# The MLP of a hybrid encoder block: three of its four two-chunk products by seven block products, activations kept in DRAM

## The chip, the cores and the metric

One core of a Trainium2 chip runs the kernel. The metric is the device time of one execution in microseconds (us), lower is better. The kernel before takes 2594.95 us, the median of three runs (2592.05 to 2595.93).

## The reference, cut to what matters

One encoder layer on 2048 rows of width 1024, all in float32. The last line of the block, the MLP, is what changes:

```python
h = rmsnorm(x, norm_mix_g); proj = h @ w_in                  # 1024 -> 5 x 512: q, k, v, u, vg
a_out = stick_breaking_attention(q, k, v)                    # 8 heads of 64, strictly causal
b_out = spatial_gating(gelu(u), gelu(vg), ...)               # 128-row blocks
mix = concat(rmsnorm(a_out), rmsnorm(b_out))
x = x + mix @ w_out                                          # 1024 -> 1024
h = rmsnorm(x, norm_mlp_g)
act = square(relu(h @ w_up))                                 # 1024 -> 4096
x = x + act @ w_down                                         # 4096 -> 1024
return rmsnorm(x, norm_final_g)
```

## The kernel before

The 2048 rows go in four chunks of 512 (`TC`). Every product keeps float32 accuracy by splitting both operands into a high and a low part: `split` (lines 78 to 85) makes the high part on ACT (lines 81, 84) and the low part, the difference, on DVE (lines 82, 85), and `mm3` (lines 87 to 90) issues three matmuls per 128x128 by 128x512 block:

```python
def mm3(ps, lh, ll, rh, rl, first, last):
    nc.tensor.matmul(ps, lh, rh, start=first, stop=False)
    nc.tensor.matmul(ps, lh, rl, start=False, stop=False)
    nc.tensor.matmul(ps, ll, rh, start=False, stop=last)
```

The program has four kinds of work. `proj` (line 108) makes q, k, v and the gated rows of a chunk and writes q, k and v to DRAM. Its layer-norm part multiplies and adds on POOL (GpSimd, lines 225 and 226). `attention` (line 280) is a generator of 325 steps. Step i forms the scores of a block of 128 queries and 512 keys (PE, lines 309 and 310), two sigmoids (ACT, 315 and 317), a scan and a product (DVE, lines 320 and 321 on the diagonal, 323 and 324 off it), and for earlier blocks four transposes (PE, 334), a split of the transposed weights `aT` and two products with v (PE, 352 and 353). 128 of its 320 blocks are on the diagonal and shorter. The third kind is the class `Block` (line 398): `out_operands` and `out` (the output projection, rows of x added on DVE at line 478), `turn` (line 491: RMS norm, then transposes into `hT`), and the MLP by `up` (line 507) and `down` (line 543).

The MLP of a chunk goes by 16 groups of 256 hidden columns. `up` loads the weights of a group, splits them, multiplies them with `hT` (24 matmuls per 128 hidden columns), and leaves the split activations in SBUF; `down` multiplies them at once with `w_down` and adds the products to the rows `y` on DVE (line 557). Nothing of the MLP goes through DRAM. `middle` (line 588) chains them.

The order around the change is written out at the end of the function (lines 638 to 686) with `together(main, side, ratio)`: `side`, the attention, moves `ratio` steps for each step of `main`, a step being 12 matmuls of a product.

```python
together(proj([0, 1], [here, Rows(spx, ps_x, "x", 0)], sp, True))
...
together(proj([2], [here], sp, False), side, R_A)      # R_A = 0.65
together(proj([3], [here], sp, True), side, R_A)
...                                                    # out and turn of chunk 0 and 1: R_O = 0.8
last = together(blocks[0].middle(), side, R_B)         # R_B = 1.0
...
assert together(middle, side, R_B) is OPEN             # the attention ends inside chunk 1's MLP
...                                                    # chunks 2 and 3 then share one Block and its weights
```

So chunk 0 and a part of chunk 1 run their MLP beside the attention, and chunks 2 and 3 run theirs together afterwards. Loads and stores are issued on SP's queue (`nc.sync`). Each engine's instructions are put in order when the program is built; tiles of one name share a fixed number of buffers (`bufs`).

## Time and profile before

| | |
|---|---|
| median of three runs | 2594.95 us (2592.05 to 2595.93) |
| the profiled execution: first to last instruction (span) | 2591.2 us; the page gives no other time for it |
| instructions | 33154 |
| DMA | 299.99 MB, mean 116 GB/s |

A share in the page is busy time over the span, averaged over stages that differ. A matmul's listed time is its latency; matmuls overlap, so the distance between two starts is what one costs. Windows (stretches of the span) show for each engine the busy time and, in brackets, the number of instructions, then the granted TensorE clock as a share of full speed, the busy share of the DMA engines, and GB/s.

### The profile page before, as it was taken

What the parts mean: (1) busy time and instruction counts of PE and PEld (TensorE: products, weight loads), DVE (VectorE), ACT (ScalarE), POOL (GpSimd) and SP (SyncE); (2) the same over time, 40 slices, a digit from 0 to 9 for tenths busy, and PEclk for the clock granted to TensorE, in tenths of its full rate; (3) what the DMA queues carried; (4) which work ended last, traced back from release to release, by engine and by line L of the source; (5) the groups of instructions that cost most, each with busy time, mean ns of one, the idle gap of its engine ahead of it and who ended that gap; (6) DMA issues with size and microseconds to landing.
All of it is one profiled execution on the core that took longest, in us unless ns stands there. A gap on an engine that the chain in (4) does not pass through costs nothing.

```text
span 2591.2 us, 33154 instructions
## 1 busy us (share of the span) xinstructions
PE 2521.4 (97%) x11904; PEld 2047.3 (79%) x11904; DVE 1795.8 (69%) x2722; ACT 1223.2 (47%) x2306; POOL 164.4 (6%) x175
## 2 busy tenths in 40 slices
PE   7999998999999999999999999999999999999998
PEld 5788776777878888777788888877888888888886
DVE  6634688778888888899888888875833434344445
ACT  6314456455556555565655555663533232222222
POOL 3200022010000000011000000011100000000000
PEclk9999999999999999999999999999999999999999
DMA  6246756556443444346343334343311111111111
GB/s 211 97 127 207 217 158 193 155 175 192 130 123 118 122 123 122 122 123 196 98 121 116 117 117 122 108 145 98 131 54 47 46 49 49 49 49 45 45 45 66
DMA packets 160229, 299.99 MB, mean 116 GB/s; under 512 B 16576, under 2 KB 32960, under 8 KB 160064
## 3 DMA queue, kind: packets, MB, share of 16 engines
q1 hardware_dynamic: 155760, 295.77, 37.1%
q10 hardware_dynamic: 4304, 2.10, 0.3%
q8 instruction: 94, 1.54, 0.3%
q14 instruction: 71, 0.58, 0.1%
HBM read 255.86 MB, written 41.94 MB: 115 GB/s over the span
## 4 chain that ended last, share of the span: by engine, by line
PE 70%; DVE 20%; DMA 3%; issue 3%; ACT 3%; POOL 1%; SPq 0%; DVEq 0%; POOLq 0%; ACTq 0%
PE mm L89 20%; PE mm L90 20%; PE mm L88 20%; DVE pr L323 4%; DVE y L557 3%; PE tr L334 3%; DVE aT L82 2%; DVE b L324 2%; PE av L352 2%; PE av L353 2%; PE z L309 1%; PE z L310 1%; DVE pr L320 1%; DMA st<-in_w_in 1%; DVE w L82 1%
## 5 line engine op out<-in xcount | busy, mean ns | idle before, releaser
L81 ACT ACTIVATE w<-w_st 128x512 fp32r<-128x512 f32 x384 | 242.7, 634 | 457.1 <-PE mm L90 442.9
L82 DVE TENSOR_TENSOR w<-w_st,w 128x512 fp32r<-128x512 f32 x384 | 259.9, 685 | 163.8 <-ACT w L81 163.7
L90 PE MATMUL mm<-hT,w 128*128 128x512 f32 (+1 forms) x816 | 309.7, 379 | 0.0
L89 PE MATMUL mm<-hT,w 128*128 128x512 f32 (+1 forms) x816 | 308.7, 378 | 0.0
L88 PE MATMUL mm<-hT,w 128*128 128x512 f32 (+1 forms) x816 | 308.6, 378 | 0.1
L88 PE MATMUL mm<-w,act 128*128 128x512 f32 x768 | 300.8, 392 | 2.1 <-DVE y L557 1.4
L90 PE MATMUL mm<-w,act 128*128 128x512 f32 x768 | 301.6, 393 | 0.0
L89 PE MATMUL mm<-w,act 128*128 128x512 f32 x768 | 300.6, 391 | 0.0
L557 DVE TENSOR_TENSOR y<-mm,y 128x512 f32<-128x512 f32 x384 | 257.7, 684 | 49.9 <-PE mm L90 49.3
L323 DVE TENSOR_TENSOR_SCAN pr<-kk,pr,zeros 128x513 f32<-128x513 f32 x192 | 245.4, 1279 | 33.8 <-ACT kk L315 33.7
L315 ACT ACTIVATE kk<-z 128x512 f32<-128x512 f32 (+2 forms) x320 | 168.7, 527 | 176.4 <-PE z L310 122.3
L535 ACT ACTIVATE rl<-mm 128x512 f32<-128x512 f32 x128 | 76.5, 597 | 327.1 <-PE mm L90 326.9
L82 DVE TENSOR_TENSOR aT<-tr,aT 128x512 fp32r<-128x512 f32 (+1 forms) x320 | 190.7, 596 | 6.9 <-ACT aT L81 6.9
L334 PE MATMUL tr<-ident,b 128*128 128x128 f32 x1088 | 180.2, 275 | 6.1 <-DVE b L324 2.6
L81 ACT ACTIVATE aT<-tr 128x512 fp32r<-128x512 f32 (+1 forms) x320 | 172.7, 540 | 21.0 <-PE tr L334 20.4
L88 PEld LDWEIGHTS mm<-hT,w 128*128 128x128 f32 x816 | 154.0, 189 | 30.3 <-DVE y L557 0.5
L82 DVE TENSOR_TENSOR act<-rl,act 128x512 fp32r<-128x512 f32 x96 | 65.8, 686 | 161.0 <-ACT act L81 159.9
L90 PEld LDWEIGHTS mm<-hT,w 128*128 128x128 f32 x816 | 153.5, 188 | 29.4
L89 PEld LDWEIGHTS mm<-hT,w 128*128 128x128 f32 x816 | 153.5, 188 | 29.2
L88 PEld LDWEIGHTS mm<-w,act 128*128 128x128 f32 x768 | 144.6, 188 | 36.2 <-DVE y L557 3.7
L317 ACT ACTIVATE b<-z 128x512 f32<-128x512 f32 (+2 forms) x320 | 169.9, 531 | 0.0
L90 PEld LDWEIGHTS mm<-w,act 128*128 128x128 f32 x768 | 144.1, 188 | 31.3
(185 smaller groups left out, 5272.0 us busy)
## 6 DMA issues: line engine op xcount, KB each, us to landing
w_st<-in_w_up SPq DMA_DIRECT2D x192, 256.0 KB, 2.8
w_st<-in_w_down SPq DMA_DIRECT2D x192, 256.0 KB, 2.8
kt<-k_d SPq DMA_DIRECT2D x160, 256.0 KB, 4.7
st<-in_w_in SPq DMA_DIRECT2D x60, 512.0 KB, 5.2
vt<-v_d SPq DMA_DIRECT2D x80, 256.0 KB, 3.0
w_st<-in_w_out SPq DMA_DIRECT2D x64, 256.0 KB, 3.4
st<-in_x_t SPq DMA_DIRECT2D x16, 512.0 KB, 4.8
st<-in_x SPq DMA_DIRECT2D x16, 512.0 KB, 4.8
```

The costliest lines, as they stand in the source:

```text
L81: nc.scalar.activation(hi, src, AF.Copy)
L82: nc.vector.tensor_tensor(lo, src, hi.bitcast(F32), ALU.subtract)
L88: nc.tensor.matmul(ps, lh, rh, start=first, stop=False)
L89: nc.tensor.matmul(ps, lh, rl, start=False, stop=False)
L90: nc.tensor.matmul(ps, ll, rh, start=False, stop=last)
L315: nc.scalar.activation(kk[:, :L], z[:, :L], AF.Sigmoid, scale=-QK_SCALE)
L317: nc.scalar.activation(b[:, :L], z[:, :L], AF.Sigmoid, scale=QK_SCALE)
L323: nc.vector.tensor_tensor_scan(pr[:, ::-1], kk[:, ::-1], zeros, carry[tb], ALU.mult, ALU.add)
L324: nc.vector.tensor_tensor(b, b, pr[:, 1:TC + 1], ALU.mult)
L334: nc.tensor.transpose(tr[:, tb * P:(tb + 1) * P], bs[tb][:, j * P:(j + 1) * P], ident)
L535: nc.scalar.activation(rl, ps, AF.Relu)
L557: nc.vector.tensor_tensor(y[:, hs], ps, y[:, hs], ALU.add)
```

## The change

The MLP works on two chunks at once (0 and 1, then 2 and 3). Of its four products, the up product of chunks 0 and 1 stays as it was (`up_plain`, beside the attention); the down product of chunks 0 and 1 and both products of chunks 2 and 3 are made from seven block products on a 2x2 split of both operands, instead of eight, with sums of blocks formed before (`seven`, `seven_left`) and after (on PSUM results). The activations' seven block operands are written to DRAM (`s_d`) and read back for `down_seven`; so are the rows `y` (`y_d`), `hT` of chunks 2 and 3 (`h_d`) and its sums (`th_d`). The attention's rates change, and it now ends inside `up_plain`.

```diff
-    R_A, R_O, R_B = 0.65, 0.8, 1.0
+    R_A, R_O, R_U = 1.0, 1.0, 1.75
...
-    FG, RL_BUFS, ST_BUFS, W_BUFS = 2, 2, 4, 9
-    class Block:      # out_operands, out, turn, up, down, middle
...
+    NG = 4
+    ORDER = (0, 5, 6, 4, 1, 3, 2)
+    ORDER_D = (0, 5, 1, 6, 4, 3, 2)
+    class Out:        # operands, product, turn: as before, in fewer and larger pieces; y goes to y_d
...
+    def seven(rm, b11, b12, b21, b22, spare):
+        t1, t2, t4n = spare
+        nc.gpsimd.tensor_tensor(t1, b12, b11, ALU.subtract)
+        nc.gpsimd.tensor_tensor(t2, b22, t1, ALU.subtract)
+        nc.gpsimd.tensor_tensor(b12, b22, b12, ALU.subtract)
+        nc.gpsimd.tensor_tensor(t4n, b21, t2, ALU.subtract)
+        return [b11, b21, b22, t4n, t1, t2, b12]
+    def seven_left(engine, a11, a12, a21, a22, spare):
+        s1, s2, s4 = spare
+        engine.tensor_tensor(s1, a21, a22, ALU.add)
+        engine.tensor_tensor(s2, s1, a11, ALU.subtract)
+        engine.tensor_tensor(a21, a11, a21, ALU.subtract)
+        engine.tensor_tensor(s4, a12, s2, ALU.subtract)
+        return [a11, a12, s4, a22, s1, s2, a21]
+    def keep_acts(p, q, a11, a12, a21, a22, rm, engine):
+        ops = seven_left(engine, a11, a12, a21, a22, ...)
+        for i, op in enumerate(ops):
+            nc.sync.dma_start(s_d[p][q // 4][i][:, q % 4, :], op)
+    def up_plain(p, hTs, rm):
+        for q in range(16):
...                    # 2 x (load, split) of w_up, 4 x 24 matmuls, relu, square
+            keep_acts(p, q, ..., rm, nc.gpsimd)
+    def sums_of_h(rm):
+        for j in range(4):
+            st = rm.raw8([2, 2, TC])
+            nc.sync.dma_start(st, h_d[j])
+            ops = seven(rm, ...)
+            for i in range(4):
+                nc.sync.dma_start(th_d[i][:, j, :], ops[3 + i])
+    def up_seven(p, rm):
+        for i in ORDER:
+            st = rm.raw8([4, TC])          # from h_d or th_d, split into hc[i] = rm.big([2, 4, TC])
...
+        for q in range(16):
+            st = rm.raw8([2, 2, 512])
+            nc.sync.dma_start(st, w_up[2 * q:2 * q + 2]...)
+            ops = seven_left(nc.gpsimd, ...)
...                    # 7 forms: split of ops[i], 12 matmuls; 5 additions on DVE from PSUM; relu, square
+            keep_acts(p, q, c11, c21, c12, u3, rm, nc.vector)
+    def down_seven(p, rm):
...                    # y of both chunks (y_d) and an accumulator stay in rm.big
+        for g in range(NG):
+            for h in range(2):
+                st = rm.big([4, D])
+                nc.sync.dma_start(st, w_down[f0 * P:(f0 + 4) * P, :]...)
+                ops.append(seven(rm, ...))                # operands of 128x1024
+            for n, i in enumerate(ORDER_D):
+                st = rm.raw8([4, TC])
+                nc.sync.dma_start(st, s_d[p][g][i])
+                for h in range(2):
+                    a, b = rm.w8([2, 2, TC]), rm.w8([2, 2, 512])
+                    split(a[:, 0], a[:, 1], st[:, 2 * h:2 * h + 2, :])
+                    split(b[:, 0], b[:, 1], ops[h][i])
+                for k in range(4):
+                    for tb in range(NTB):
+                        passes(tb, k)                     # 3 matmuls
+                for tb in range(NTB):
+                    done(tb)                              # PSUM added to acc or y on DVE
...
-        blocks = [Block([c], [here], [here], mp) for c in range(2)]
...
+            rm = Room(op, ps_mm, dict(big=4, w8=3, t4=7, ys=1), hp)
+            for c in range(2):                            # Out of chunks 0, 1 beside attention, R_O
...
+            rm = Room(upp, ps_mm, dict(big=4, w8=4, t4=9), hp)
+            main = up_plain(0, hTs, rm)
+            if together(main, side, R_U) is OPEN:
+                together(main)
...
+        rm = Room(mlp, ps_b, dict(big=7, w8=5, raw8=2, t4=8))
+        for c in (2, 3):
+            o = Out(c, rm, c - 2)
+            together(o.operands()); together(o.product()); together(o.turn())
+        sums_of_h(rm)
+        together(down_seven(0, rm))
+        together(up_seven(1, rm))
+        together(down_seven(1, rm))
```

## Rows read from the trace of the kernel before

**Rows 1.** Page, busy time and share of each engine.
```profile
PE 2521.4 (97%) x11904; PEld 2047.3 (79%) x11904; DVE 1795.8 (69%) x2722; ACT 1223.2 (47%) x2306; POOL 164.4 (6%) x175
```

**Rows 2.** Windows, all engines: PE, PEld, DVE, ACT, POOL busy (instructions), clock, DMA share, GB/s.
```profile
262.00:1705.00 1443.00, 1403.04 (x6910) 1136.32 (x6908) 1234.46 (x1849) 836.89 (x1656) 93.81 (x88) 0.99 0.46 138
1705.00:2592.00 887.00, 872.36 (x3927) 712.78 (x3925) 427.56 (x667) 282.22 (x500) 28.89 (x36) 1.00 0.19 66
2100.00:2200.00 100.00, 100.00 (x435) 81.38 (x434) 43.92 (x66) 25.40 (x42) 0.00 (x0) 1.00 0.14 48
0.00:10.00 10.00, 2.45 (x6) 1.98 (x7) 3.70 (x6) 4.64 (x5) 1.62 (x11) 1.00 0.81 275
60.00:70.00 10.00, 4.86 (x12) 2.87 (x12) 9.11 (x13) 5.57 (x8) 7.46 (x6) 0.79 0.33 105
```

**Rows 3.** Windows of line 88 alone (a third of the products): PE, PEld.
```profile
262.00:1705.00 1443.00, 549.19 (x1419) 268.21 (x1418) 0.99 0.46 138
1705.00:2592.00 887.00, 489.81 (x1263) 237.21 (x1262) 1.00 0.19 66
```

**Rows 4.** Timeline of PE at 1205 us: start, listed time; one attention step and one step of main.
```profile
1205.68 0.39 PE L309 MATMUL z<-kt,qt 128*128 128x512 f32 x1
...
1207.08 0.39 PE L88 MATMUL mm<-w,hT 128*128 128x512 f32 x1
...
1209.85 0.39 PE L309 MATMUL z<-kt,qt 128*128 128x512 f32 x1
```

**Rows 5.** Windows of DVE, 262 to 1705 us, for the tiles w, y and act in turn.
```profile
262.00:1705.00 1443.00, 192.02 (x280) 0.99 0.46 138
262.00:1705.00 1443.00, 187.47 (x276) 0.99 0.46 138
262.00:1705.00 1443.00, 51.23 (x68) 0.99 0.46 138
```

**Rows 6.** Groups by line and shape: count, busy us, mean ns, idle before.
```profile
L82 DVE TENSOR_TENSOR w_in<-st,w_in 128x1024 fp32r<-128x1024 f32 x60 | 76.1, 1274 | 25.3 <-ACT w_in L81 24.9
L81 ACT ACTIVATE w_in<-st 128x1024 fp32r<-128x1024 f32 x60 | 63.2, 1058 | 27.8 <-DMA st<-in_w_in 21.9 <-PE mm L90 5.6
L557 DVE TENSOR_TENSOR y<-mm,y 128x512 f32<-128x512 f32 x384 | 257.7, 684 | 49.9 <-PE mm L90 49.3
L226 POOL TENSOR_TENSOR vn<-vn,ln_b_t 128x512 f32<-128x512 f32 x12 | 18.1, 1508 | 0.7
```

**Rows 7.** Timelines of DVE, then POOL, at 435 to 444 us: start, duration.
```profile
436.25 0.69 DVE L220 BATCH_NORM_STATS2 ln_st<-vn 128x6 f32<-128x512 f32 x1
...
440.21 1.66 DVE L208 TENSOR_TENSOR gelu_t<-gelu_t,vn 128x512 f32<-128x512 f32 x1
441.79 2.32 DVE L82 TENSOR_TENSOR w_in<-st,w_in 128x1024 fp32r<-128x1024 f32 x1
...
435.70 1.68 POOL L225 TENSOR_TENSOR vn<-vn,ln_g_t 128x512 f32<-128x512 f32 x1 [0.66 <-DVE vn L224]
437.45 1.30 POOL L226 TENSOR_TENSOR vn<-vn,ln_b_t 128x512 f32<-128x512 f32 x1
...
439.92 1.40 POOL L225 TENSOR_TENSOR vn<-vn,ln_g_t 128x512 f32<-128x512 f32 x1 [0.66 <-DVE vn L224]
441.40 1.62 POOL L226 TENSOR_TENSOR vn<-vn,ln_b_t 128x512 f32<-128x512 f32 x1
```

**Rows 8.** DMA issues: count, KB each, median us from issue to landing.
```profile
st<-in_x_t SPq DMA_DIRECT2D x16, 512.0 KB, 4.8
k_d<-qkv_st SPq DMA_DIRECT2D x32, 256.0 KB, 3.5
```

**Rows 9.** Instructions on yx and hT after 1690 us: duration min/median/max, first to last start.
```profile
L468 SPq DMA_DIRECT2D yx<-in_x x4: 424/430/432, 1728.0 to 1729.4; - x4
L410 ACT ACTIVATE rl<-yx x4: 1040/1042/1057, 1821.3 to 1828.5; 128x1024 bf16<-128x1024 f32 x4
L412 DVE SCALAR_TENSOR_TENSOR act<-yx,n_r,gmlp_t x4: 1276/1282/1285, 1824.0 to 1834.8; 128x1024 f32<-128x1024 f32 x4
...
L88 PE MATMUL mm<-hT,w x32: 387/389/500, 1704.1 to 1744.1; 128*128 128x512 f32 x32
```

More of the change, by code (lines that the diff above doesn't have):

```diff
@@ L276, in block_kernel @@
     kk_n = [0]
-    R_A, R_O, R_B = 0.65, 0.8, 1.0
+    steps = [0]
+    R_A, R_O, R_U = 1.0, 1.0, 1.75
     def attention(cs):
@@ L479, in group @@
+                    if half == 1 and part == 0:
+                        nc.sync.dma_start(y_d[c][:, tb, :], ys[:, tb, :])
                     yield
-            yield from group(0, 1, bm, ws or self.out_weights(0, 1), rbs)
-            pssq = pl.ps()
+            yield from group(0, 1, self.bm, self.rbs)
+            pssq = rm.ps()
             for tb in range(NTB):
-                nc.tensor.matmul(pssq[:, tb:tb + 1], total[:, tb * P:(tb + 1) * P], ones, start=True, stop=True)
-            ra = rsqrt_mean(self.mp, pssq[:, :NTB], NTB, SBW, "ra")
+                nc.tensor.matmul(pssq[:, tb:tb + 1], self.total[:, tb * P:(tb + 1) * P], ones, start=True, stop=True)
@@ new lines, in product, with turn @@
+            yield from group(1, 1, self.bm, self.rbs)
+            yield from group(1, 0, self.am, ras)
+        def turn(self):
+            rm = self.rm
+            gain = rm.t4([D])
+            nc.sync.dma_start(gain, gmlp.broadcast_to([P, D]))
+            kept = self.place is None
+            self.hT = [rm.big([2, 4, TC], F32R) if kept else rm.raw8([4, TC]) for _ in range(2)]
+            for tb in range(NTB):
+                src = self.ys[:, tb, :]
+                nrm = rm.t4([D])
+                ssq = rm.small("n2_ssq")
+                nc.scalar.activation(nrm, src, AF.Square, accum_out=ssq)
+                r = rsqrt_mean(rm.pool, ssq, 1, D, "n2")
+                nc.vector.scalar_tensor_tensor(nrm, src, r[:, 0:1], gain, ALU.mult, ALU.mult)
+                ts_ = slice(tb * P, (tb + 1) * P)
@@ L588, in middle @@
-        def middle(self):
-            acts = yield from self.up(0)
-            for fg in range(NG - 1):
-                after = yield from self.up(fg + 1)
-                yield from self.down(fg, acts)
-                acts = after
-            return self.down(NG - 1, acts, True)
+                    h = self.hT[kk]
+                    if kept:
+                        split(h[:, 0, :, ts_], h[:, 1, :, ts_], ps)
+                    else:
+                        nc.scalar.activation(h[:, :, ts_], ps, AF.Copy)
@@ new lines, in turn @@
+                yield
+            if not kept:
+                for kk in range(2):
+                    nc.sync.dma_start(h_d[:, :, kk, self.place, :].rearrange("j p t -> p j t"), self.hT[kk])
+    def seven(rm, b11, b12, b21, b22, spare):
[5 more added lines that the diff above has]
+        return [b11, b21, b22, t4n, t1, t2, b12]
@@ L671, in block_kernel @@
-        together(blocks[1].turn(0), side, R_O)
-        middle = blocks[1].middle()
-        assert together(middle, side, R_B) is OPEN
-    with tc.tile_pool(name="ext", bufs=1, side="right", reuse_waits="tile") as ext, \
-            tc.tile_pool(name="ps_b", bufs=5, space=PSUM, reuse_waits="tile") as ps_b:
-        there = Place(ext, ps_b, "x", 4)
-        block = Block([2, 3], [here, there], [here, there], mp)
-        together(block.out_operands(1))
-        last = together(middle)
-        together(block.out(1))
-        together(block.out_operands(0))
-        together(last)
-        together(block.turn(1))
-        together(block.out(0))
-        together(block.turn(0))
-        together(together(block.middle()))
+        with tc.tile_pool(name="hp", bufs=1, reuse_waits="tile") as hp:
+            hTs = []
+            with tc.tile_pool(name="op", bufs=1, reuse_waits="tile") as op:
+                rm = Room(op, ps_mm, dict(big=4, w8=3, t4=7, ys=1), hp)
+                for c in range(2):
+                    while steps[0] < 16 * (c + 1) * (c + 2) + NTB + 1:
+                        next(side)
+                    o = Out(c, rm, None)
+                    together(o.operands(), side, R_O)
+                    together(o.product(), side, R_O)
+                    together(o.turn(), side, R_O)
+                    hTs.append(o.hT)
+            with tc.tile_pool(name="upp", bufs=1, reuse_waits="tile") as upp:
+                rm = Room(upp, ps_mm, dict(big=4, w8=4, t4=9), hp)
+                main = up_plain(0, hTs, rm)
+                if together(main, side, R_U) is OPEN:
+                    together(main)
+                for _ in side:
+                    pass
@@ new lines, in block_kernel @@
+    mm_stack.close()
+    with tc.tile_pool(name="mlp", bufs=1, reuse_waits="tile") as mlp, \
+            tc.tile_pool(name="ps_b", bufs=8, space=PSUM, reuse_waits="tile") as ps_b:
+        rm = Room(mlp, ps_b, dict(big=7, w8=5, raw8=2, t4=8))
+        for c in (2, 3):
+            o = Out(c, rm, c - 2)
+            together(o.operands())
+            together(o.product())
+            together(o.turn())
+        sums_of_h(rm)
+        together(down_seven(0, rm))
+        together(up_seven(1, rm))
+        together(down_seven(1, rm))
```

438 lines of the change are left out of this document (254 added, 184 removed).

## The prediction

> **What bounds the kernel now.** I began with the busy times: TensorE is busy for 97% of the span, the next engine (DVE) for 69% [rows 1]. A matmul's listed time is a latency, so I took the real cost from a window in which nothing else happens: 435 matmuls in 100.00 us, 0.2299 us each, at full clock [rows 2]. With that price I split the span at 262 us, where the attention starts, and 1705 us, where it ends. Line 88 is a third of all products: 1263 of them after 1705 us [rows 3], times 3, times 0.2299, is 871 us. 64 are half as wide (the first group of each chunk goes by half chunks), which takes off 21; transposes and the attention's last products add 13. So 863 of those 887 us are work and about 24 idle. Between 262 and 1705 us, 1419 x 3 x 0.2299 = 979 us, less 21 for half-wide ones. An attention step costs TensorE 1.40 us, and a step of twelve matmuls 2.77 [rows 4]; for a block on the diagonal I estimate 0.92 from the widths. 192 x 1.40 + 128 x 0.92 = 387. With 20 for transposes: 1365 of 1443 us, 78 idle, 5.4%. In that stretch DVE is busy for 1234 us and POOL for 94 [rows 2]. So the kernel is bound by TensorE throughout, tightly after the attention and with DVE close behind during it. Matmuls that go away are worth their full price, if the others are fed as well as now.
>
> **What is removed.** Each product of two chunks is 2 x 32 x 8 x 3 = 1536 matmuls. By seven blocks it is 16 x 84 = 1344 for the up product and 4 x 7 x 48 = 1344 for a down product. Three of them: 576 matmuls x 0.230 = **132 us**. Loads of weights also fall (w_up and w_down are read twice, not three times), which is worth nothing, since they lie under matmuls.
>
> **The stretch with attention.** It now holds the products of chunks 2 and 3's projection (960 matmuls, 24 of them before 262 us), two output projections (384) and some 115 of the 128 steps of the plain up product (1380): (of 325 attention steps 80 + 44 go beside the first two kinds, and 201 / 1.75 = 115). 2700 x 0.2299 = 621, plus 387 and 20: **1030 us** of TensorE. DVE: from 1234 I take the MLP's share of weights, y and act [rows 5], without the 64 weight and y pieces and 8 norms of the two output projections (58 us): 373, some 345 after overlap of neighbours. The plain up product adds 29 splits of 128x1024 at 1.27 [rows 6], 37. That gives 926 us.
>
> But POOL gets four additions per group of 256 columns, 58 in this stretch, and they are not beside DVE's work: at 440.21 and 441.79 us two DVE instructions with two SBUF operands took 1.66 and 2.32 us instead of 0.69 and 1.27, each until POOL's addition had ended, while one with a single SBUF operand ran in 0.69 under POOL's [rows 7, 6]. At 1.30 us each they are 75 us, beside the 94 that POOL had. DVE plus POOL is 926 + 169 = 1095 us, more than TensorE's 1030. Bounds: at the idle share of before, 1030 / 0.946 = 1089; if DVE and POOL together reach only the share they had before (1328 of 1443, 92%), 1190. Part of DVE's work reads PSUM (the split of aT), which leaves it free, and 92% was not what held the kernel then, so I take 1120, a third of the way.
>
> The Trainium skill (SBUF — State Buffer, Who interferes with whom) says that a DVE instruction with two SBUF inputs and a GpSimd one that reads SBUF exclude each other for the whole instruction, and that one with at most one SBUF input doesn't. By it in full, every split from SBUF, scan and product would be serial with POOL, and the stretch would be the upper 1190; without it, 1089. The rows above show both halves, at two instructions.
>
> **The stretch after it.** Work: 13 steps of the plain up product, two output projections and three products of 1344 are 4572 matmuls, 1051 us, plus 14 for transposes: 1065. What the steady loops need, against a step of the seven: in `down_seven` one of 48 matmuls, 11.1 us. ACT makes 4 x 1.06 = 4.2, DVE 4 x 1.27 + 4 x 0.68 = 7.8 [rows 6]; 1 MB of activations and 0.6 of weights in 11.1 us are 144 GB/s, where 275 were reached [rows 2]. In `up_seven` a group is 84 matmuls, 19.3 us, with DVE 16 x 0.68 = 10.9, POOL 5.2 and 2.8 MB, 147 GB/s. So these are hidden, but not the places where a stage starts on what the last one left:
> - Start of chunk 2's rows, whose buffers lie where the plain up product's lay, and the step from chunk 2 to 3: 5 each. The bound below is 0.
> - **The sums of hT.** After chunk 3's last product TensorE has only its transposes: the norm chain (addition 0.68, square 1.04, power 0.55, scaling 1.28 and transposes [rows 6, 9]) about 5.5; hT stored (1 MB, about 6 by 4.8 for 512 KB [rows 8]), read back 6, four POOL additions 5.2, stored 3.5 [rows 8]. With two `raw8` buffers that goes round twice before a buffer takes the first activations: load 6, split 2.3. Sum 49. If the loads of `down_seven` get a buffer first, only about 15: before, yx was loaded at 1728 us, while matmuls that stand earlier in the program ran until 1744 [rows 9], so instructions do run ahead; but not past others for buffers of their own name, as far as I can see. I take 35, nearer the long chain.
> - `down_seven` to `up_seven`: seven operands, 1 MB each through two buffers, into buffers that the rows y give back only after their store: 8 (0 to 20).
> - `up_seven` to `down_seven`: y and w_down, 8 MB at 275 GB/s are 29 us, and their buffers come free one by one during the last group of 19.3: 10 (5 to 20).
> - POOL's eight additions of 128x1024 per quarter, 2.6 us each, hold up low parts: in a burst DVE passes one 1.2 us split per 3.8 us, where TensorE wants one per 2.8. Two such tiles ahead cover most of it; 10 in all (0 to 50).
> - End of the last rows, as before: 12. Clock: where TensorE was busy for 4.86 of 10 us the granted clock was 0.79 [rows 2], full in steady stretches; after three gaps a few us each, 10.
>
> Idle: 90 (35 to 140), stretch 1155.
>
> **Sum.** 262 + 1120 + 1155 = 2537 us of span, against 2591.2. The median of the runs is 3.75 above that span, so the prediction is **2541 us**, 2.1% faster: 132 less in matmuls, given back by about 66 more idle at the seams and 12 in the attention stretch.
>
> **Rivals.**
> *All hidden* (0.20). DVE and POOL cause no more idle time than before, and the transfers at the seams run ahead: 262 + 1089 + 1100 + 4 = 2455. For it: before, loads ran ahead of the program's order [rows 9]. Against: the sums of hT are a true chain, store, load, addition, store.
> *DVE and POOL become the bound* (0.17), slower. Its place is the plain up product, whose group of eight steps and 14 attention steps gives TensorE 40 us and DVE plus POOL about 39. The attention's own chain (scores, sigmoid, scan, product, transposes, split) crosses DVE three times per step, so each 1.3 us block falls into a chain that TensorE waits for. It turns the sign when the stretch exceeds 1174 us, that is when DVE and POOL are kept to below 93.3% of it. At 90% it is 1217, and bursts in `down_seven` at their upper bound add 40: 262 + 1217 + 1195 + 4 = 2678; I put it at 2600 to 2680. For it: 92% is all that the two had before. Against: then they were not the bound.
> *The seams at their upper bounds* (0.12): 262 + 1120 + 1205 + 4 = 2591, no measurable change. If the transfers through DRAM fell short, it would look like this.
> The forecast's own case, 2500 to 2585, has 0.51. That the matmuls don't go away, though the code counts them so, is no case: they are issued as counted.
>
> **Numbers.** A difference of 0.2%, about 5 us, is what a measurement of this kernel can tell from none. Faster: the forecast, all hidden and half of the third rival, 0.77. Same, the other half, 0.06. Slower, 0.17. The range stops inside the hidden case on one side and the slower one on the other: 2475 to 2620, about 0.1 left out on either side.
>
> **What would show it.** Right: 576 matmuls fewer among the products; 0.230 us from start to start in `down_seven`; gaps of TensorE of 30 us and more ahead of the first of its matmuls, with POOL and SP's stores in between; in the plain up product DVE near 90% and PE within 6% of full, with POOL's additions of `seven_left` near 1.3 to 1.6 us and the DVE instruction beside them stretched. Wrong: line 88's matmuls further apart in the steady loops, the plain up product over 45 us per group, or DVE waiting for loads of `s_d` rather than for ACT.

## The result: 11.6% slower, and the profile after

Timed on the same chip, four runs each, the changed kernel takes 2894.51 us (2890.89 to 2898.22) against 2593.56 (2592.05 to 2595.93): ratio 1.116, 95% interval 1.1145 to 1.1178. Forecast were 2541 us and a range up to 2620. The profiled execution has a span of 2896.5 us. I read it as I read the one of before: busy times first, then stages.

The busy line of the page answers to [rows 1]:

```profile
PE 2521.2 (87%) x11136; PEld 1991.7 (69%) x11136; DVE 1887.4 (65%) x2424; ACT 1264.4 (44%) x2144; POOL 589.7 (20%) x379
```

768 PE instructions fewer, as counted (576, and 192 because the first group of a chunk no longer goes by half chunks). Yet TensorE is at 87% instead of 97%, and no other engine is near full: DVE, the next, is at 65%, and in none of the stages below over 85%. So nothing has become "the bound"; TensorE waits. Where, the windows tell, one for each stage: attention beside the projection, beside the output projections of chunks 0 and 1, beside the plain up product; that product's rest; output projections of chunks 2 and 3; the sums of hT; first down product; seam; up product by blocks; seam; second down product. Columns as in [rows 2].

```profile
262.00:606.00 344.00, 317.99 (x1581) 256.01 (x1581) 284.36 (x434) 190.68 (x369) 46.46 (x42) 0.99 0.58 168
606.00:805.00 199.00, 175.10 (x839) 136.92 (x837) 168.79 (x251) 114.97 (x228) 27.41 (x26) 0.93 0.55 167
805.00:1549.00 744.00, 650.33 (x2926) 493.08 (x2924) 527.59 (x645) 381.83 (x756) 108.47 (x70) 0.92 0.40 113
1549.00:1618.00 69.00, 50.57 (x195) 38.72 (x194) 6.11 (x6) 13.33 (x20) 4.96 (x4) 0.87 0.19 61
1618.00:1777.00 159.00, 111.67 (x496) 90.50 (x496) 70.89 (x102) 56.10 (x97) 25.60 (x26) 0.84 0.56 213
1777.00:1826.00 49.00, 0.00 (x0) 0.00 (x0) 0.62 (x1) 2.31 (x3) 29.08 (x21) 0.50 0.74 256
1826.00:2140.00 314.00, 306.99 (x1323) 251.36 (x1324) 244.44 (x245) 118.95 (x123) 90.77 (x32) 0.98 0.38 140
2140.00:2180.00 40.00, 11.75 (x39) 8.41 (x39) 29.89 (x31) 18.50 (x26) 12.06 (x10) 0.62 0.70 255
2180.00:2557.00 377.00, 338.59 (x1328) 263.41 (x1326) 165.30 (x249) 143.20 (x250) 99.76 (x60) 0.93 0.37 130
2557.00:2580.00 23.00, 13.37 (x41) 9.67 (x42) 13.92 (x8) 6.31 (x7) 17.79 (x7) 0.70 1.00 357
2580.00:2896.00 316.00, 300.27 (x1304) 245.67 (x1302) 239.88 (x252) 114.39 (x121) 86.10 (x34) 0.98 0.36 133
```

The same view of line 87 alone (the first of `mm3`'s three matmuls in the changed file, so a third of the products) gives each stage's products; times three, times 0.2299 us, they are its work:

```profile
805.00:1618.00 813.00, 213.91 (x512) 0.92 0.38 109
1826.00:2140.00 314.00, 172.51 (x443) 0.98 0.38 140
2180.00:2557.00 377.00, 183.82 (x442) 0.93 0.37 130
```

The first down product needs 443 x 3 x 0.2299 = 306 us and takes 314: the seven-block loop runs as forecast. The up product by blocks takes 377 for 305. The plain up product takes 813 for 353 of products and 197 attention steps. For the price of a step I took the first MLP of the kernel before (windows of PE, of its line 88 and then of line 309, one per attention step):

```profile
650.00:1160.00 510.00, 196.69 (x512) 1.00 0.40 121
650.00:1160.00 510.00, 44.75 (x122) 1.00 0.40 121
```

That is (510 - 353) / 122, about 1.28 us each, the little idle time of that stretch included. 197 steps are then 252 us, so some 208 us of the 813 are idle. By the same count, with 13 to 16 us of transposes for each two output projections, the projection loses 30, the first output projections 40, the second ones 55, the sums 49, the two seams 32 and 13. The stretch with attention ended at 1549 us instead of the forecast 1382, the stretch after it took 1347 instead of 1155. So 167 us of the miss lie in the first and 192 in the second.

**The plain up product.** Two timelines of one group, SP's stores of activations (L553) and loads of `w_up` (L564) and POOL's sums; then ACT's split of the loaded weights, and the products before and after the pause:

```profile
1016.42 8.20 SPq L553 DMA_DIRECT2D s_d<-t  x5
1024.67 0.45 SPq L564 DMA_DIRECT2D t<-in_w_up  x1
...
1016.48 1.79 POOL L542 TENSOR_TENSOR t<-t 128x512 f32<-128x512 f32 x1 [16.00 <-ACT t L556]
...
1019.92 2.19 POOL L544 TENSOR_TENSOR t<-t,t 128x512 f32<-128x512 f32 x1
1022.07 1.72 POOL L545 TENSOR_TENSOR t<-t,t 128x512 f32<-128x512 f32 x1
...
1029.08 1.06 ACT L79 ACTIVATE w<-t 128x1024 fp32r<-128x1024 f32 x1 [0.75 <-DMA t<-in_w_up]
...
1014.37 0.39 PE L89 MATMUL mm<-big,w 128*128 128x512 f32 x1
1030.19 0.50 PE L87 MATMUL mm<-big,w 128*128 128x512 f32 x1
```

The next group's load starts at 1024.67, behind stores that wait for POOL, and lands at 1029. Between 1014.37 and 1030.19 no product runs, attention steps alone do. This comes once per group: 813 / 16 = 51 us instead of 40. Which of the things in this picture holds the load (the queue, the stores, POOL, or the buffer that it goes into, one of nine named `t` that activations, sums and weights share), the view does not say. The runs and SP's waits below do.

### The profile page after: what moved, and what is told of

Same layout as the page of the kernel before. It is cut to its first block, busy times and chain, and to the rows that moved or that the text cites. A ratio compares the mean times of both kernels' runs of the same rounds, so it can differ in the third digit from the quotient of the medians.

```text
span 2896.5 us, 30864 instructions
## 1 busy us (share of the span) xinstructions
PE 2521.2 (87%) x11136; PEld 1991.7 (69%) x11136; DVE 1887.4 (65%) x2424; ACT 1264.4 (44%) x2144; POOL 589.7 (20%) x379
## 5 line engine op out<-in xcount | busy, mean ns | idle before, releaser
L87 PE MATMUL mm<-big,w 128*128 128x512 f32 x960 | 401.2, 418 | 63.0 <-ACT w L79 62.8
L89 PE MATMUL mm<-big,w 128*128 128x512 f32 x960 | 394.6, 413 | 34.4 <-DVE w L80 34.3
L87 PE MATMUL mm<-w,w 128*128 128x512 f32 x896 | 348.0, 394 | 58.6 <-ACT w L79 58.6
L88 PE MATMUL mm<-big,w 128*128 128x512 f32 x960 | 394.7, 411 | 0.0
L88 PE MATMUL mm<-w,w 128*128 128x512 f32 x896 | 354.9, 396 | 15.8 <-DVE w L80 14.1
L89 PE MATMUL mm<-w,w 128*128 128x512 f32 x896 | 352.7, 394 | 0.0
L87 PEld LDWEIGHTS mm<-big,w 128*128 128x128 f32 x960 | 193.4, 202 | 116.8 <-ACT w L79 76.2
L80 DVE TENSOR_TENSOR aT<-tr,aT 128x512 fp32r<-128x512 f32 (+1 forms) x320 | 190.3, 596 | 118.4 <-ACT aT L79 118.1
L89 PEld LDWEIGHTS mm<-big,w 128*128 128x128 f32 x960 | 190.5, 198 | 89.5 <-DVE w L80 47.6
L80 DVE TENSOR_TENSOR w<-raw,w 128x1024 fp32r<-128x1024 f32 (+1 forms) x176 | 214.3, 1232 | 50.6 <-ACT w L79 50.4
L87 PEld LDWEIGHTS mm<-w,w 128*128 128x128 f32 x896 | 169.7, 190 | 97.1 <-ACT w L79 62.0
L334 PE MATMUL tr<-ident,b 128*128 128x128 f32 x1088 | 198.1, 292 | 29.0 <-DVE aT L80 13.9
L88 PEld LDWEIGHTS mm<-big,w 128*128 128x128 f32 x960 | 192.0, 200 | 41.8
L80 DVE TENSOR_TENSOR w<-t,w 128x1024 fp32r<-128x1024 f32 (+1 forms) x128 | 136.4, 1075 | 122.0 <-ACT w L79 121.6
L88 PEld LDWEIGHTS mm<-w,w 128*128 128x128 f32 x896 | 170.9, 191 | 57.5 <-DVE w L80 21.7
L353 PE MATMUL av<-aT,vt 128*128 128x512 f32 (+1 forms) x320 | 140.6, 439 | 76.1 <-DVE aT L80 71.3
L79 ACT ACTIVATE w<-t 128x1024 fp32r<-128x1024 f32 (+1 forms) x128 | 113.5, 898 | 192.0 <-issue 83.8
L89 PEld LDWEIGHTS mm<-w,w 128*128 128x128 f32 x896 | 171.0, 191 | 35.3
L334 PEld LDWEIGHTS tr<-ident,b 128*128 128x128 f32 x1088 | 142.9, 150 | 65.4 <-DVE aT L80 17.6
```

Source lines behind the costliest of these rows:

```text
L79: nc.scalar.activation(hi, src, AF.Copy)
L80: nc.vector.tensor_tensor(lo, src, hi.bitcast(F32), ALU.subtract)
L87: nc.tensor.matmul(ps, lh, rh, start=first, stop=False, skip_group_check=more)
L88: nc.tensor.matmul(ps, lh, rl, start=False, stop=False, skip_group_check=more)
L89: nc.tensor.matmul(ps, ll, rh, start=False, stop=last, skip_group_check=more)
L334: nc.tensor.transpose(tr[:, tb * P:(tb + 1) * P], bs[tb][:, j * P:(j + 1) * P], ident)
```

## The experiments

Sixteen kernels, each beside runs of the kernel before on the same chip (2592.94 to 2594.89). One run each unless said, so differences under about 5 us tell nothing.

### The plain up product: buffers, order, or the engine of the sums

**up_own**

```diff
-                st = rm.t4([8, P])
+                st = rm.pool.tile([P, 8, P], F32, name="wst", bufs=3)
-                rm = Room(upp, ps_mm, dict(big=4, w8=4, t4=9), hp)
+                rm = Room(upp, ps_mm, dict(big=4, w8=4, t4=6), hp)
```

> Edit: in the plain up product (805 to 1618 us of the changed kernel, 813 us for some 561 us of TensorE work) the loads of w_up get three buffers of their own instead of places in the shared ring of nine, which shrinks to six. The order in which the code asks for loads and stores stays. Theory A (the weights come late because a load has to wait for a place in the shared ring or stands on SP behind stores that wait for the sums): with places of their own the loads lose one of their two waits; if the ring is the one that ends last, the plain up product falls by 80 to 150 us, to about 2770 in all; if the place in SP's queue ends last, by under 30 us. Theory B (POOL's sums beside DVE hold DVE up, and attention with it): nothing in this edit touches that, so 2895 within 10 us.

**up_first** (up_own, and the load two ahead asked for behind the split)

```diff
+        raw = [load(0), load(1)]
...
-                st = rm.pool.tile([P, 8, P], F32, name="wst", bufs=3)
-                nc.sync.dma_start(st, w_up[2 * q + fi])
+                st = raw.pop(0)
...
+                if 2 * q + fi + 2 < 32:
+                    raw.append(load(2 * q + fi + 2))
```

> Edit: as the run with buffers of their own for the loads of w_up, and besides the load of the weights two ahead is asked for before the stores of a group, right behind the split that uses a buffer up. Theory A (late weights): both waits of a load are gone, the pauses of the products of about 12 to 16 us per group go, and the plain up product falls by 100 to 180 us of its 813, to 2715 to 2795 in all; nothing but attention's own rate is left in it. Theory B (POOL's sums hold DVE and attention up): within 20 us of 2895, for POOL and DVE have the same work.

**up_dve**

```diff
-            keep_acts(p, q, cs[0][:, 0, :], cs[0][:, 1, :], cs[1][:, 0, :], cs[1][:, 1, :], rm, nc.gpsimd)
+            keep_acts(p, q, cs[0][:, 0, :], cs[0][:, 1, :], cs[1][:, 0, :], cs[1][:, 1, :], rm, nc.vector)
```

> Edit: in the plain up product the four sums of a group go on DVE instead of POOL; loads and stores as in the changed kernel. Theory B (the lock): POOL's 64 operations of 1.5 to 2.2 us that stand beside DVE's go, and DVE gets 64 of 0.69 us, 44 us in all; if POOL's operations hold DVE up for their whole time, the plain up product falls by about 60 us, to 2835. Theory A (late weights): the stores are ready some 4 us earlier in each of 16 groups, so a gain of at most 64 us where the store is what the load waits for, less up to 44 us of more work on DVE: 2875 to 2920. The two overlap little; the gap of the products before a group's first matmul tells more: under A it stays over 8 us.

Measured: up_own 2769.19 us, up_first 2768.82, up_dve 2857.12. The same nine places of SBUF, divided otherwise, are worth 125 us; asking earlier adds nothing. The group of ACT's splits of these weights, of the changed kernel and then of up_own (from the start of the stage to its end), shows the wait for the load going:

```profile
L79 ACT ACTIVATE w<-t 128x1024 fp32r<-128x1024 f32 x32 | 34.4, 1074 | 25.8 <-DMA t<-in_w_up 25.8
```
```profile
L79 ACT ACTIVATE w<-wst 128x1024 fp32r<-128x1024 f32 x32 | 34.9, 1090 | 0.5 <-DMA wst<-in_w_up 0.5
```

ACT's 25.8 us are less than TensorE's loss, since only the idle time right before such a split is listed, and attention's work on ACT lies in the rest of the wait. up_dve's 37 us lie between its two expectations, so the total decides nothing. The pause does: in up_dve's PE timeline no product starts between 1004.97 and 1020.55 us nor between 1052.35 and 1067.09, 15 us in each group as in the changed kernel, while in up_own no pause over 4 us is left between 960 and 1120 us. That is theory A's sign. The granted clock in the stage goes up with it, from 0.92 to 1.00. With own buffers a load is asked for more than a group ahead (one issued at 955.04 us is split at 1016.94; in the changed kernel 4 to 8 us lie between), and the stores before it in the queue cost nothing.

The edit moves two things at once, the buffer and the place in SP's queue, since the order on SP differs between the two traces. What SP itself waited for in the changed kernel, 805 to 1549 us (stores L553, loads L564: us in total, times, longest), tells which of the two held the load when it ran:

```profile
SPq L553 <- ACT t L556: 203.8, 33, 12.7
...
SPq L564 <- DVE t L514: 1.9, 1, 1.9
```

The loads wait for 1.9 us of their own, the stores for 204 on ACT's squares and 85 on POOL's sums. By this view it was the place behind the stores that held the load, not a buffer still in use. That the shared buffers put it into this place is inferred from up_own, which changes nothing but buffers. The either-or of the expectation, under 30 us if the queue ends last, was too neat.

### POOL's sums beside DVE

**no_sums** (on up_own; `up_plain` passes `None` as the engine, which leaves out the four sums)

```diff
+        if engine is None:
+            ops = [a11, a12, a12, a22, a21, a22, a21]
+        else:
...
```

> Edit: on the kernel with own buffers for the weights alone (up_own, 2769): the four sums per group of the plain up product are left out, and plain activations are stored in their places, so this kernel leaves out POOL's 64 operations of that stage; loads, stores and products stay. Theory B (POOL's operations beside DVE's stretch these: the low parts of the weights take 1.68 us at the mean instead of 1.22, attention's product of 128x512 0.80 instead of 0.69, and DVE is what bounds the stage): 25 to 40 us less, 2730 to 2745. Rival (the stage is bound by TensorE and by attention's own chain): within 10 us of 2769.

**own_dve** (up_own and up_dve together)

> Edit: on up_own (2769) the four sums of the plain up product go on DVE, 64 operations of 0.69 us, 44 us. Leaving POOL's sums out gave 24 us. If DVE bounds the stage, those 24 come back but 44 are added: 2780 to 2795. If TensorE's own waits bound it, and POOL hurts only by stretching the operations that stand in attention's chain, 2745 to 2765.

Measured: 2745.57 and 2752.14 us against up_own's 2769.19; no_sums just short of theory B's lower end. DVE's groups in the stage, of up_own and then of no_sums:

```profile
L323 DVE TENSOR_TENSOR_SCAN pr<-kk,pr,zeros 128x513 f32<-128x513 f32 x144 | 189.5, 1316 | 51.7 <-ACT kk L315 51.5
L324 DVE TENSOR_TENSOR b<-b,pr 128x512 f32<-128x512 f32 x144 | 113.8, 791 | 7.2
L80 DVE TENSOR_TENSOR aT<-tr,aT 128x512 fp32r<-128x512 f32 x161 | 108.9, 677 | 7.7 <-ACT aT L79 7.5
L80 DVE TENSOR_TENSOR w<-wst,w 128x1024 fp32r<-128x1024 f32 x32 | 53.6, 1674 | 5.6 <-ACT w L79 5.6
```
```profile
L323 DVE TENSOR_TENSOR_SCAN pr<-kk,pr,zeros 128x513 f32<-128x513 f32 x144 | 184.3, 1281 | 61.0 <-ACT kk L315 60.6
L80 DVE TENSOR_TENSOR aT<-tr,aT 128x512 fp32r<-128x512 f32 x162 | 109.9, 678 | 9.2 <-ACT aT L79 9.0
L324 DVE TENSOR_TENSOR b<-b,pr 128x512 f32<-128x512 f32 x144 | 98.9, 688 | 7.2
L80 DVE TENSOR_TENSOR w<-wst,w 128x1024 fp32r<-128x1024 f32 x32 | 38.9, 1216 | 5.6 <-ACT w L79 5.6
```

The split and the product with two SBUF operands lose 14.7 and 14.9 us beside POOL, the scan 5.2; the split of aT, which reads PSUM, loses nothing (677 and 678 ns). 35 us of DVE, 24 us of the kernel. The Trainium skill (SBUF — State Buffer, Who interferes with whom) says that a DVE instruction with two SBUF inputs contends with a GpSimd one that reads SBUF, and that one with at most one SBUF input doesn't. The trace agrees, but for the scan only weakly: it has two SBUF inputs too and loses 35 ns at the mean, where the product loses 103. The 24 us are not POOL's alone beyond doubt, since no_sums also takes two tiles fewer per group from the ring of six. But own_dve keeps these tiles, gives DVE 44 us more work and is 17 us faster. So the part of theory B that has DVE full does not hold. What is left is the second expectation of own_dve, that POOL hurts by lengthening operations that stand in attention's chain; the times fit it, the chain itself was not followed.

### The up product by blocks

**up7_pool**

```diff
-            keep_acts(p, q, c11, c21, c12, u3, rm, nc.vector)
+            keep_acts(p, q, c11, c21, c12, u3, rm, nc.gpsimd)
```

> Edit: in the up product by blocks (2180 to 2557 us of the changed kernel, 23.5 us per group for 19.3 of matmuls) the four sums of the activations go on POOL instead of DVE. Theory C (the low parts of the next group's weights stand on DVE behind these four sums of 0.69 us, so the third pass waits 2.1 us, and after it the products run for some matmuls at the lower clock): the wait of 2.1 us goes and with it the slow matmuls, 2.5 to 4 us per group, 40 to 65 us in all, to 2830 to 2855. Rival (the group is held by the chain relu, square, split on ACT, or by the ring of buffers and the stores, which POOL's slower sums release later): within 10 us of 2895, or slower by up to 4 us per group, 2960.

**up7_ahead** (`weights` loads a group's weights and makes their sums; what it returns splits one operand)

```diff
+            if q < 15:
+                after = weights(q + 1)
             form(2, b5, False)
+            if q < 15:
+                after(0)
+                after(5)
...
             keep_acts(p, q, c11, c21, c12, u3, rm, nc.vector)
```

> Edit: in the up product by blocks the next group's weights are asked for ahead of the last form of a group, and their first two operands are split ahead of the four sums of this group's activations; the buffers stay as they are. Theory C (the low parts of the weights stand on DVE behind these sums): the wait of 2.1 us per group and the slow matmuls behind it go, 2.5 to 4 us in each of 16 groups, 40 to 65 us, to 2830 to 2855. Rival (a group is held by its ring of buffers, which the stores free, as it was when the sums went to POOL and the time rose by 105 us): within 15 us of 2895.

DVE's timeline in the changed kernel at a group's end (L542 to L545 are the four sums, L80 the low parts of the next weights), then PE's:

```profile
2318.17 0.69 DVE L542 TENSOR_TENSOR t<-t 128x512 f32<-128x512 f32 x1 [1.36 <-ACT t L556]
...
2320.11 0.69 DVE L545 TENSOR_TENSOR t<-t,t 128x512 f32<-128x512 f32 x1
2320.71 1.29 DVE L80 TENSOR_TENSOR w<-t,w 128x512 fp32r<-128x512 f32 x2
...
2322.05 0.80 PE L89 MATMUL mm<-big,w 128*128 128x512 f32 x1 [2.09 <-DVE w L80]
2322.64 0.63 PE L87 MATMUL mm<-big,w 128*128 128x512 f32 x1
2323.07 0.63 PE L88 MATMUL mm<-big,w 128*128 128x512 f32 x1
```

And the windows around the pause:

```profile
2322.00:2325.00 3.00, 2.95 (x7) 2.37 (x8) 2.40 (x4) 0.26 (x1) 1.88 (x1) 0.50 0.36 87
2325.00:2340.00 15.00, 15.00 (x65) 12.13 (x65) 3.38 (x5) 3.76 (x6) 4.79 (x4) 0.99 0.28 104
```

PE waits 2.09 us for a low part that stands behind the sums, and in the whole stage 31.3 us for it, in 15 groups. Its source was there before: POOL's sums of these weights had ended at 2306 us, and ACT made the high parts from 2318.04 on. After the wait the granted clock is 0.50 (1.2 GHz) for some 3 us, and matmuls start 0.43 us apart instead of 0.23. The first addition of a group on DVE (x16) gives the mean group, in the changed kernel and in up7_ahead:

```profile
L630 DVE TENSOR_TENSOR t<-mm,t x16: 679/692/693, 2186.5 to 2541.3; 128x512 f32<-128x512 f32 x16
```
```profile
L635 DVE TENSOR_TENSOR t<-mm,t x16: 675/675/693, 2185.2 to 2473.4; 128x512 f32<-128x512 f32 x16
```

354.8 / 15 = 23.7 us per group, and 288.2 / 15 = 19.2, which is the 84 matmuls. That is 66 us of the stage from the first group to the last. up7_ahead measured 2841.27, a gain of 53: some of it comes back behind, where the first matmul of the last down product now waits 17.84 us in one piece. Theory C holds, inside its interval. up7_pool measured 2999.51, 105 slower, beyond the rival's 2960. A POOL timeline of it shows the turn:

```profile
2414.41 1.26 POOL L545 TENSOR_TENSOR t<-t,t 128x512 f32<-128x512 f32 x1
2415.63 1.26 POOL L542 TENSOR_TENSOR t<-raw 128x512 f32<-128x512 f32 x1
```

The weights' sums (L542 on `raw`) now follow the activations' (L545 on `t`) at once, so on one engine the next weights wait until this group's activations are done; PE then waits 7.7 us per group for their split. A group took 30.7 us. By POOL's time alone, eight additions of 1.26 to 1.73 us, it would have fitted into 19.3; its order decides.

### The seams

**sums_later** (`sums_of_h` yields after each of its four parts)

```diff
-        sums_of_h(rm)
-        together(down_seven(0, rm))
+        sums = sums_of_h(rm)
+        for n, _ in enumerate(down_seven(0, rm)):
+            if n in (34, 41, 48, 55):
+                next(sums)
```

> Edit: the sums of the normed rows of chunks 2 and 3 (the 49 us at 1777 to 1826 us of the changed kernel in which no matmul stands) are made inside the first down product, one of their four parts after each quarter step, instead of ahead of it. Theory D (the chain of loads, four POOL operations of 1.26 us and stores is on the path only because nothing else stands beside it, and the steady down product covers it): 40 to 49 us less, 2845 to 2855; the down product keeps its 314 us within 10. Rival (POOL's 16 sums and the two shared buffers that they take hold up the down product's operands, whose own sums are POOL's too): at most 20 us less, 2875 to 2895.

**seam** (the first `w_up` load ahead of the seven operands, these by halves)

```diff
-        for i in ORDER:
-            st = rm.raw8([4, TC])
...
+            for j in range(0, 4, 2):
+                st = rm.t4([2, TC])
+                nc.sync.dma_start(st, src[:, j:j + 2, :])
```

> Edit: the up product by blocks asks for its first weights ahead of its seven operands from the rows, and the operands come in halves through the ring of eight small buffers instead of through the two of 1 MB. Theory E (the 32 us of idle TensorE at 2140 to 2180 us come from the first weights' load behind seven operands in two buffers): 15 to 28 us less, 2867 to 2880. Rival (the pause is the 7 MB of operands themselves, which the DMA has to bring whatever the order): within 8 us of 2895.

Measured: 2871.30 and 2888.33 us, 23 and 6 less. The first matmul of the first down product, in the changed kernel and in sums_later:

```profile
1826.34 1.65 PE L87 MATMUL mm<-w,w 128*128 128x512 f32 x3 [49.34 <-ACT w L79]
```
```profile
1784.04 1.65 PE L87 MATMUL mm<-w,w 128*128 128x512 f32 x3 [12.23 <-ACT w L79]
```

The start moves by 42 us, but the first matmul of the up product by blocks only from 2173.33 to 2147.68, 26 us: the down product, in which POOL's 16 sums now lie, became longer by the rest, 16 us, where theory D allowed 10. Between theory and rival. In seam the one wait of 27.8 us for the weights became waits of 11.3 and 2.4 for operands, 3.1 and 1.6 for weights, and the operands trickled in: the rival's forecast, within 8 us, is met. A gain of 6 is hardly more than the noise of one run.

### All together, and the rest

**mended** (up_own, up7_ahead, sums_later, seam)

> Edit: the three edits of this call and the weights' own buffers in the plain up product together. If each of the four stages has a cause of its own, the gains add up: 125 of the own buffers as measured, 40 to 49, 40 to 65 and 15 to 28, so 2630 to 2675. If the gains meet (less work hidden in one stage coming out in the next, above all in the ring of small buffers that three of the stages share), 2690 to 2750. In no case under the 2594 of the kernel before, which stands 37 us below the lower end.

Measured 2689.75. The four gains as measured add up to 207, to 2687: they add, so what one edit wins does not come back in another's stage. The sum misses the range that I had given for this case by 15 us, since sums_later and seam brought 23 and 6 where I had expected at least 40 and 15; up_own and up7_ahead lay inside their ranges.

**paced**

```diff
-    R_A, R_O, R_U = 1.0, 1.0, 1.75
+    R_A, R_O, R_U = 1.0, 1.0, 1.55
```

> Edit: on the kernel with all four edits (mended, 2690): attention goes along at 1.55 steps per step of the plain up product instead of 1.75, so that its 197 steps last to the product's end (128 steps) instead of ending some 92 us ahead of it. Theory F (while attention runs at 1.75, DVE is the bound, 0.83 busy at the mean beside TensorE's 0.94, and after it DVE idles): spreading gains 15 to 30 us, 2660 to 2675. Rival (the sum of the work of TensorE is the bound in that stage, and the pace moves nothing): within 8 us of 2690; if part of attention is left over for the end of the stage, where nothing lies beside it, up to 20 us more.

**pairs** (operands of chunk 3 during the products of chunk 2, turn of chunk 2 during the products of chunk 3)

```diff
+        side = o3.operands()
+        for n, _ in enumerate(o2.product()):
+            if n in (4, 8):
+                next(side)
+        side = o2.turn()
+        for n, _ in enumerate(o3.product()):
+            if n in (2, 4, 6, 8):
+                next(side)
```

> Edit: on mended: the output projections of chunks 2 and 3 (176 us from the last up product to the first down product for 88 us of products and some 20 us of transposes) overlap: the operands of chunk 3 are made during the products of chunk 2, and the rows of chunk 2 are normed and turned during the products of chunk 3. Theory G (the stage loses its time in the chains load, split, product, norm, turn, which stand one behind the other without attention to fill them): 20 to 40 us less, 2650 to 2670. Rival (the loads, 212 GB/s in this stretch of the changed kernel, set the stage): within 8 us of 2690.

**both**

> Edit: paced and pairs together on mended, the best of what was tried here. The gains add, being in different stages: 2620 to 2655 by theories F and G, 2690 by their rivals. Slower than the kernel before (2594) in either case, by 1 to 4%: the removed products are worth 132 us, and the stages that the change makes still lose more than that in starts and ends that no other work covers.

Measured: paced 2705.09, 15 slower; pairs 2666.04, 24 faster (theory G); both, in four runs, 2675.66 (2672.70 to 2680.47), ratio 1.0313, interval 1.0296 to 1.0330: about the sum of the two as measured, and so above the 2620 to 2655 of the theories. The chains that pairs overlaps are the waits in these groups of PE in the changed kernel, 1618 to 1777 us (transposes of the rows at L519 and of b at L439):

```profile
L87 PE MATMUL mm<-w,big 128*128 128x512 f32 x128 | 52.7, 411 | 19.3 <-ACT w L82 19.3
...
L519 PE MATMUL mm<-ident,t 128*128 128x128 f32 x64 | 8.7, 288 | 8.3 <-DVE t L514 8.3
L439 PE MATMUL mm<-ident,t 128*128 128x128 f32 x32 | 7.4, 421 | 20.2 <-DMA t<-b_d 20.2
```

Theory F fell: in mended attention's last product with v starts at 1456 us, not at 1400, so there was less to spread than I had said; at 1.55 the last scores start at 1497 us, when the product is nearly through (its last result is read at 1501 us). The rival had named this case, up to 20 us more for attention left over at the end.

**before_150, before_125** (the kernel before, none of the change; 1.25 in the second)

```diff
-    R_A, R_O, R_B = 0.65, 0.8, 1.0
+    R_A, R_O, R_B = 0.65, 0.8, 1.5
```

> Edit on the kernel before, with nothing of the change in it: attention goes along with the MLP at 1.5 steps per step instead of 1.0, so it ends earlier and the rest of the MLP runs alone. The work is the same. Theory H (attention packed closer beside the same products costs more than its work, since DVE, 0.87 busy at 1.0, becomes the bound or the small waits no longer find a product to fill them; this is what is left of the loss in the plain up product, where 197 steps stand beside 512 triples): the first MLP (650 to 1160 us) takes 61 steps more and grows by more than their 78 us, the second gives only these 78 back; 20 to 60 us slower in all. Rival (the pace is free, the rest of the loss belongs to the plain up product itself): within 8 us of 2594.

> Edit on the kernel before: attention's pace beside the MLP 1.25 instead of 1.0. By theory H the loss grows with the pace: 5 to 30 us slower, and less than half of that at 1.5 if the point at which DVE fills lies between (DVE's 446 us of 510 at pace 1.0 would fill at about 1.2). Rival: within 8 us of 2594.

**slow_side** (pairs, with R_U = 1.0)

> Edit: on pairs (2666) attention's pace in the plain up product is 1.0 instead of 1.75: 128 steps beside its 512 triples and some 69 steps alone behind it. By the work alone the product with 128 steps would take 353 + 164 = 517 us. Theory H: it comes within 20 us of that, while at 1.75 it stood 80 us above its work; the 69 steps alone run at DVE's rate, 2.4 to 3 us each, 165 to 210 us where they cost 1.28 beside products, so the whole is 2720 to 2790. Rival (the stage has a cost of its own for each group, whatever the pace): the product takes 570 us or more.

Measured: 2630.44 us at 1.5 and 2615.23 at 1.25, against 2594.89: 36 and 20 slower with the same work in another order. Theory H holds, and the loss lies where it put it: with 1.5, 4983 PE instructions stand between 650 and 1705 us instead of 5151, and the time after 1705 us grows from 886 to 923 us. More than half of the loss is there at 1.25, so nothing speaks for a point at which DVE fills; two runs don't rule it out. slow_side took 2692.85, below the 2720 to 2790 of theory H. Its plain up product (window of line 87, then of line 309, one per attention step), and the attention alone behind it:

```profile
805.00:1360.00 555.00, 201.36 (x512) 1.00 0.44 134
```
```profile
805.00:1360.00 555.00, 48.87 (x131) 1.00 0.44 134
...
1400.00:1500.00 100.00, 21.29 (x46) 0.91 0.44 95
```

131 steps and 512 triples are 353 + 168 = 521 us of work in 555, 34 idle. In up_own 198 steps (the same view of its line 309) and the same triples stood in 686 us, 80 idle:

```profile
805.00:1491.00 686.00, 74.13 (x198) 1.00 0.44 129
```

So of the 80 some 46 go with the pace. That is nearer theory H, which asked for 537 us at most, than the rival, which asked for 570; a step beyond the first 131 cost (686 - 555) / 67 = 2.0 us there, alone it costs 100 / 46 = 2.2. By these two prices, attention's steps hardly share TensorE with the products any more at this density.

## Why the prediction was wrong

**Removed matmuls: right.** The count and the price hold: 0.23 us a matmul in the first down product, and in the up product once it is mended.

**"The stretch with attention", 1120 us: 1287 measured.** The work term was right (1287 less 253 idle is 1034, for 1030). The idle term failed: I bounded it by engines' busy times alone (1089 to 1190), and asked of `w_up` nothing but that it be split. The step that failed is in "DVE plus POOL": it named the engines that could be full and put the loads of `w_up` at nothing without a reason. It never asked which stores a load stands behind and whose buffers it shares. 125 us of the loss in the plain up product (here and in its rest after attention) go back to that, shown by up_own. I had written the sign of it among what would show the prediction wrong, over 45 us per group, and gave the cause behind it no price. The sign that I had named for the forecast, DVE near 90% in the plain up product, did not come: it was busy for 527.59 of 744 us beside attention, 71%. What is left in that product, 80 us, fits POOL's stretching of DVE (24 us, no_sums) and a pace of 1.75 where 1.0 had stood (some 46 us by slow_side; 20 and 36 us for 1.25 and 1.5 in the kernel before); that the two add was not shown. The 70 us idle in the two stretches before it, at a pace of 1.0 where 0.65 and 0.8 had stood, stay open. I had priced an attention step at 1.40 or 0.92 us from a kernel in which it stands beside 12 matmuls or more, and carried the price to one where 12 matmuls share the engine with 1.75 steps.

**"So these are hidden", the steady loops: half right.** `down_seven` is hidden, with idle 8 us of 314. `up_seven` was 23.7 us per group for 19.3: by summed busy times DVE had room (10.9 of 19.3), but its four sums stood ahead of the next weights in its own order. The wait of 2.1 us, and the 1.5 that some 3 us at half the clock lose, are most of the 4.4. Order on an engine, not load. up7_ahead shows it: with the order changed a group takes 19.2.

**"Clock", 10 us for three gaps: too small.** The pauses came in every group, and the granted clock was 0.92 beside attention in the plain up product and 0.93 in the up product by blocks.

**Seams.** The sums of hT took 49 us without a matmul. The chain that I had added up to 49 step by step is there, down to its end: ACT waits 46.65 us for the first activations (`raw<-s_d`), whose buffers the sums give back. That the figure agrees so well is in part luck, since my 49 began with the norm chain, which lies ahead of these 49 us. I had then talked it down to 35 on the ground that loads might run ahead. Down to up was 32 against an upper bound of 20; I had let the seven operands come during the last steps before. Up to down, 13 for 10, and the bursts of POOL in `down_seven`, under 10, were right. "Start of chunk 2's rows, 5 each": 55 us idle in 159. There I had looked at buffers, and not seen that these two output projections, which the kernel before laid between MLP steps, now stand alone with their chains; letting them overlap gave back 24.

**Of the rivals** the one on the slow side had the place right for about half of the miss, the plain up product, and for most of the loss there the wrong mechanism: with its mechanism at work and nothing else, the loss would have been about the 24 us that no_sums took off up_own. Each of my cases took it for granted that what fits into the busy times comes in time. The range was too narrow on the slow side for that, not through chance: the waits above, in the plain up product, in `up_seven`, at the seams and in the projections of chunks 2 and 3, had small prices or none.

**Two slips in the working** change little: the idle terms that I listed after the attention add up to 95 us and not to 90, and the first two of [rows 5] are y and then w, while only their sum is used.

**Beyond that** the four edits together with pairs stand at 2666 us, a single run, 72 above the kernel before in spite of 132 us fewer matmuls. Nothing that I tried beats the kernel before. By pieces: the pace and POOL's sums in the plain up product (80 us), the projections of chunks 2 and 3 without cover, the seams of 12 to 30 us at each start of a stage. What the first two stretches with attention (projection, first output projections, 30 and 40 us idle) would give back at the old pace was not tried.

## What to carry to other kernels

Price a new loop by three questions, not by busy times alone: which buffer each load takes, who must give it back first, and what stands ahead of the load in its queue; what stands ahead of the next operand on the engine that makes it; and what else is left to run when it waits. Here a ring that weights share with activations on their way to DRAM went with the next load standing behind the last stores; three buffers taken out of the nine were worth 125 us. And a generator that runs beside another is cheap at a pace that leaves the other's matmuls between its steps: closer packed, its steps cost nearly what they cost alone.

## What the runs showed of the hardware

A pause of TensorE of 2.1 us was followed by about 3 us at a granted clock of 0.50 (1.2 GHz), with matmuls 0.43 us apart. A group with one such pause took 4.4 us more than its matmuls, twice the length of the pause. In the 49 us without any matmul the granted clock was 0.50 as well. POOL's additions of 128x512 took 1.26 us beside an idle DVE (in the sums of hT) and up to 2.2 beside a busy one (in the plain up product). The stretching goes both ways: beside them DVE's split of 128x1024 took 1674 ns at the mean instead of 1216.
